# One rate for all four quarters: 16.4 units of product between the mixers' steps instead of 12.25, 14.25, 15.25 and 19.25

## The chip, the cores and the metric

The kernel runs on one core of a Trainium2 chip. The metric is the device time of one execution in microseconds (us). The program is built from Python: a kernel file issues instructions for five engines (TensorE, here PE; VectorE, DVE; ScalarE, ACT; GpSimd, POOL; SyncE, SP, which issues nearly all DMAs), and a scheduler decides in which order they stand in each engine's queue.

## The reference

One layer of a hybrid decoder on 2,048 prompt tokens and 8 single-token samples, D = 1024. Three mixers read one input projection and share one output projection; a SwiGLU follows.

```
h = rmsnorm(x, norm_mix);  p = h @ w_in                      # 1024 -> 31 column tiles of 128 (and 12 columns)
y_a = gated DeltaNet(p_a)     # 6 heads of 64, chunks of 64: u, w by a triangular solve, then s = s*g + k_dec^T v_new
y_b = RWKV-7(p_b)             # 6 heads: state update with a vector-valued decay
y_c = HGRN2(p_c)              # 4 heads, chunks of 64: o = q*exp(b) @ s + att @ v
x = x + concat(y_a, y_b, y_c) @ w_out                        # 8 input tiles of 128: 3 from A, 3 from B, 2 from C
h = rmsnorm(x, norm_ffn)
x = x + (silu(h @ w_gate) * (h @ w_up)) @ w_down             # 2816 = 22 tiles of 128
y = rmsnorm(x, norm_final)
```

All states after the prompt and after the sample step are returned too. Everything is float32; a product is made of three passes over halves that are rounded apart (`hi`, `lo`).

## The kernel before, in words

**Quarters.** The prompt's columns are cut into four quarters of 512 (the last has the 8 samples as well, 520). In names of tiles and below, quarters are numbered 0 to 3.

**Products.** `gemm()` in `emit` is one long generator: the input projections of quarters 0 to 3 (31 tiles each, PSUM tiles `psp`), then for each quarter in turn the output projection (`out_proj`, 8 tiles, `pso`), the gate and up products (`pfg`, `pfu`) and the down products (`pd`) in `ffn`. It yields the number of matmul rows of 512 columns that it has just issued, the unit of what follows: 24 for a tile of a projection, 48 for a gate and up pair, 12 for a tile of a down product. All in all there are 10,176 units. The input projections end at 2,976, and output projection and feed-forward of a quarter take 1,776: those of quarter 0 begin at 2,976, of quarter 1 at 4,752, of quarter 2 at 6,528, of quarter 3 at 8,304. Each matmul row of a product reads one weight tile and one 512-wide tile of inputs; three PSUM banks (pool `pg`) hold products in the making. In quarter 0 each weight is also split into its two halves on ACT and DVE and stored for the other quarters.

**Mixers.** A unit is one pair of heads of one mixer in one quarter, called g (DeltaNet, units 0 to 2), r (RWKV, 0 to 2) or h (HGRN2, 0 and 1) with quarter and unit: `h20` is the first HGRN2 unit of quarter 2. `gdn`, `rwkv` and `hgrn` return two generators, `first()` and `second()`; every `yield` in them ends a step, and `NEXT` passes the unit on to the next of four stages (preparation; the triangular inverse; the recurrence over 8 chunks; output and norm). At most 1, 1, 2 and 1 units are in the four stages (`ROOM`). At its end a unit writes a tile of 128 x 512 to memory (`store_mix`, into `s_mix`). In quarter 2 the eight units of the sample step (`gs`, `rs`, `hs`) join as side units in the last stage.

**What ties the two together.** `out_proj(q)` loads the eight tiles of `s_mix[q]` (`mxs`, from `g` 0 to 2, `r` 0 to 2, `h` 0 and 1), splits them on ACT and DVE, and multiplies them with `w_out`; tiles 6 and 7 come from `h` 0 and 1, whose units are the last of their quarter. Their last stage is `gated_norm`: a product `po_h` on PE, a sum over squares, a norm, a gate, the store.

**Who sets the order.** `Driver.turn` takes every live unit one step further; then it adds the quarter's rate to `due` and issues products until as many units are made:

```
        self.due += self.rate
        while self.made < self.due and self.product():
            pass
```

`RATES[q]` is that rate while units of quarter q are started. When all units are done the rest of the products follows alone (`K.late`, with more PSUM banks and weights loaded ahead). This is the order of the program. The scheduler then sets each engine's queue from it (`schedule_with_timeline_sim`), so that steps of mixers and products may stand further apart in a queue than the rate says. Each engine works through its queue in that order.

Of the kernel before, what the change touches and what calls it, by code (L numbers as in the profile page):

```python
# [1450 lines left out]
STEP = 2  # L1451
AHEAD = 4
SLACK = 6
RATES = (12.25, 14.25, 15.25, 19.25)
ROOM = (1, 1, 2, 1)

LANES = {"A": (29, 2, "A"), "I": (1, 0, "C"), "C": (2, 0, "C"), "D": (1, 0, "D"), "P": (6, 1, "P")}
# [58 lines left out]
def emit(K):  # L1516
# [61 lines left out]
    for q in range(4):  # L1578
        D.rate = RATES[q]
        for ms, f in order:  # L1580
# [118 lines left out]
```

## Time and profile before

| what | value |
|---|---|
| median of 3 runs | 3190.97 us (3185.88 to 3197.09) |
| the profiled execution | 3185.85 us, of which the span of its instructions is 3184.1 us |
| PE busy | 3063.0 us, 96% of the span, 24,812 matmul records |
| DVE busy | 2189.0 us, 69% |
| ACT busy | 1196.6 us, 38% |
| granted TensorE clock, mean | 0.985 of full speed |

Busy times are sums over records. Matmuls are pipelined and the ends of their records are modelled, so what one matmul costs in a row of others is read from the distance of two starts, not from its length. A float32 matmul that is not split into halves leaves two records. The granted clock 1.00 is the level of 2.4 GHz, 0.5 that of 1.2 GHz.

### The profile page before, as it was taken

The page shows a single profiled execution, that of the slowest core. Times are in us where ns is not written, and L with a number is a line of the kernel's source. Part 1 is how long each engine was busy: PE and PEld are TensorE (multiplying, and loading weights), DVE is VectorE, ACT ScalarE, POOL GpSimd, SP SyncE. Part 2 cuts the span into 40 slices and gives each one's busy share as a digit, 9 for nine tenths or more (in the row PEclk, how much of TensorE's full clock was granted, in tenths as well). Part 3 has the DMA queues.
Part 4 walks back from the last instruction along what each step waited for, and adds up shares of the span by engine and source line. Part 5 has one row for each costly group of instructions (what it writes and reads, how often), then busy time and mean ns, then how long its engine had stood idle before and what let it go on. Part 6 is the DMA issues. An engine that isn't in the chain of part 4 may idle for free.

```text
span 3184.1 us, 62691 instructions
## 1 busy us (share of the span) xinstructions
PE 3063.0 (96%) x24812; PEld 2442.2 (77%) x24812; DVE 2189.0 (69%) x5424; ACT 1196.6 (38%) x2064; POOL 12.3 (0%) x41
## 2 busy tenths in 40 slices
PE   7999999999998999999989999999999999999998
PEld 5767767778897677677766777777777777999998
DVE  6783666677768888896978778868877653443334
ACT  5452243245324544543555334445433221221002
POOL 0000000000000000000000000000000000000000
PEclk9999999999999999999999999999999999999999
DMA  8877666657656766677764454557554465755552
GB/s 286 287 244 250 193 182 199 207 168 228 185 164 172 235 229 221 223 221 257 226 219 149 153 163 146 190 165 233 165 162 150 151 216 183 251 170 186 189 182 90
DMA packets 391971, 628.01 MB, mean 197 GB/s; under 512 B 172988, under 2 KB 177340, under 8 KB 391676
## 3 DMA queue, kind: packets, MB, share of 16 engines
q1 hardware_dynamic: 390588, 622.93, 61.4%
q8 instruction: 195, 3.19, 0.4%
q10 hardware_dynamic: 1088, 1.07, 0.1%
q14 instruction: 100, 0.82, 0.1%
HBM read 456.77 MB, written 167.14 MB: 196 GB/s over the span
## 4 chain that ended last, share of the span: by engine, by line
PE 68%; DVE 13%; DMA 11%; ACT 4%; SPq 2%; issue 2%; DVEq 0%; ACTq 0%
PE psp L377 5%; PE psp L379 5%; PE psp L378 5%; PE pfg L378 4%; PE pfg L377 4%; PE pfg L379 4%; PE pfu L377 4%; PE pfu L378 4%; PE pfu L379 4%; PE pd L377 4%; PE pd L379 4%; PE pd L378 4%; PE pso L377 1%; PE pso L378 1%; PE pso L379 1%
## 5 line engine op out<-in xcount | busy, mean ns | idle before, releaser
L377 PE MATMUL psp<-xs,w_in 128*128 128x512 f32 (+1 forms) x1240 | 448.7, 362 | 23.8 <-ACT w_in L332 9.7
L378 PE MATMUL psp<-xs,w_in 128*128 128x512 f32 (+1 forms) x1240 | 444.1, 358 | 0.3 <-DVE xs L418 0.3
L379 PE MATMUL psp<-xs,w_in 128*128 128x512 f32 (+1 forms) x1240 | 443.6, 359 | 0.0
L377 PEld LDWEIGHTS psp<-xs,w_in 128*128 128x128 f32 x1240 | 236.6, 191 | 67.9 <-ACT w_in L332 11.2
L379 PEld LDWEIGHTS psp<-xs,w_in 128*128 128x128 f32 x1240 | 236.0, 190 | 41.7 <-issue 4.5
L378 PEld LDWEIGHTS psp<-xs,w_in 128*128 128x128 f32 x1240 | 236.5, 191 | 35.4 <-issue 2.0
L606 DVE TENSOR_TENSOR x<-pd,x 128x512 f32<-128x512 f32 (+1 forms) x240 | 137.5, 582 | 104.0 <-PE pd L379 102.6
L377 PE MATMUL pfg<-xhs,w_wg 128*128 128x512 f32 x464 | 188.2, 406 | 7.3 <-ACT w_wg L332 4.8
L378 PE MATMUL pfg<-xhs,w_wg 128*128 128x512 f32 x464 | 188.8, 407 | 3.1 <-DVE xhs L564 3.1
L377 PE MATMUL pd<-u,w_wd 128*128 128x512 f32 x448 | 179.3, 409 | 10.4 <-DVE x L606 7.0
L379 PE MATMUL pfg<-xhs,w_wg 128*128 128x512 f32 x464 | 187.1, 403 | 0.1
L377 PE MATMUL pfu<-xhs,w_wu 128*128 128x512 f32 x464 | 186.5, 402 | 0.0
L378 PE MATMUL pfu<-xhs,w_wu 128*128 128x512 f32 x464 | 186.3, 402 | 0.0
L379 PE MATMUL pfu<-xhs,w_wu 128*128 128x512 f32 x464 | 185.0, 399 | 0.0
L378 PE MATMUL pd<-u,w_wd 128*128 128x512 f32 x448 | 178.9, 400 | 0.6 <-DVE u L363 0.6
L379 PE MATMUL pd<-u,w_wd 128*128 128x512 f32 x448 | 178.9, 400 | 0.0
L585 ACT ACTIVATE t<-t 128x512 f32<-128x512 f32 (+1 forms) x110 | 60.0, 546 | 281.2 <-DVE t L584 277.5
L285 ACT ACT_TABLE_LOAD x91 | 116.8, 1283 | 112.6 <-PE yv_r L275 18.9
L362 ACT ACTIVATE u<-t 128x512 fp32r<-128x512 f32 (+1 forms) x110 | 60.0, 545 | 216.7 <-DVE t L588 216.7
L482 DVE TENSOR_TENSOR p<-psp,ri 128x512 f32<-128x512 f32 (+1 forms) x155 | 89.8, 580 | 71.8 <-PE psp L379 70.5
L377 PE MATMUL pd<-u,hw_wd 128*128 128x260 f32 (+1 forms) x432 | 128.2, 307 | 3.9 <-ACT u L362 3.9
L378 PE MATMUL pd<-u,hw_wd 128*128 128x260 f32 (+1 forms) x432 | 131.3, 305 | 0.0
(648 smaller groups left out, 7318.8 us busy)
## 6 DMA issues: line engine op xcount, KB each, us to landing
w_in<-sw_in SPq DMA_DIRECT2D x186, 512.0 KB
w_wg<-sw_wg SPq DMA_DIRECT2D x72, 512.0 KB
w_wu<-sw_wu SPq DMA_DIRECT2D x72, 512.0 KB
w_wd<-sw_wd SPq DMA_DIRECT2D x68, 512.0 KB
sw_in<-w_in SPq DMA_DIRECT2D x62, 512.0 KB
s_p<-p SPq DMA_DIRECT2D x93, 256.0 KB
sw_wg<-w_wg SPq DMA_DIRECT2D x44, 512.0 KB
sw_wu<-w_wu SPq DMA_DIRECT2D x44, 512.0 KB
```

The costliest lines, as they stand in the source:

```text
L285: p = self.nc.scalar.preload_act_table_set("natural_log_exp_and_others")
L362: nc.scalar.activation(out[:, 0], src, AF.Copy)
L377: nc.tensor.matmul(ps, lhsT=hi[:, ws], rhs=xs[:, 0, xc], start=start, stop=False)
L378: nc.tensor.matmul(ps, lhsT=hi[:, ws], rhs=xs[:, 1, xc], start=False, stop=False)
L379: nc.tensor.matmul(ps, lhsT=lo[:, ws], rhs=xs[:, 0, xc], start=False, stop=stop)
L482: nc.vector.tensor_tensor(p[:, c0:c0 + cn], ps, rstd[q][:, c0:c0 + cn], ALU.mult)
L585: nc.scalar.activation(t, g, AF.Tanh, scale=0.5)
L606: nc.vector.tensor_tensor(x2[d][:, c0:c0 + cn], ps, x2[d][:, c0:c0 + cn], ALU.add)
```

## The change

The four rates become one number. The mean of the four was 15.25; nothing else is edited.

```diff
 SLACK = 6
-RATES = (12.25, 14.25, 15.25, 19.25)
+RATES = (16.4, 16.4, 16.4, 16.4)
 ROOM = (1, 1, 2, 1)
```

The driver takes 484 turns with either. When the last unit is done, 7,536 units of product have been issued before, and 7,932 now. The counts of instructions are those of before on PE (19,008) and DVE (5,426); SP issues 2,315 instead of 2,343, since fewer weights are loaded in halves at the end.

Two places show what this does to the queues. The first is PE's queue at the output projection of quarter 2: `pso2_0` to `pso2_2` are its first three tiles, `mxs2_6` and `mxs2_7` the inputs that come from `h20` and `h21`. Before, the rows stand like this:

```order
L379 MATMUL pso2_0_25295<-mxs2_5_25277,w_o_0_2_25291 128x512
L377 MATMUL pso2_0_25295<-mxs2_6_25281,w_o_0_2_25291 128x512
L378 MATMUL pso2_0_25295<-mxs2_6_25281,w_o_0_2_25291 128x512
L379 MATMUL pso2_0_25295<-mxs2_6_25281,w_o_0_2_25291 128x512
L377 MATMUL pso2_0_25295<-mxs2_7_25285,w_o_0_2_25291 128x512
L378 MATMUL pso2_0_25295<-mxs2_7_25285,w_o_0_2_25291 128x512
L379 MATMUL pso2_0_25295<-mxs2_7_25285,w_o_0_2_25291 128x512
L377 MATMUL pso2_1_25349<-mxs2_0_25257,w_o_1_2_25343 128x512
```

The products follow each other without a mixer's row between them; `po_h20` and `po_h21` (16 rows each) stand 312 and 176 rows of products ahead of the first row that reads `mxs2_6`. Now the part where the input from `h20` is first read looks like this (`oss_h20` and `sp_hs00` are sums of the norm of `h20` and of the first HGRN2 sample unit, `g30`, `g31` and `r30` units of quarter 3):

```order
L378 MATMUL pso2_2_24326<-mxs2_5_24161,w_o_2_2_24322 128x512
L703 MATMUL pi_r30_23758<-uT_r30_23756,inF0_204 32x32 x7
L274 MATMUL oss_h20_22503<-hi_oss_h20_22504,blkr_92 128x512
L703 MATMUL pi_r30_23758<-uT_r30_23756,inF0_204 32x32 x6
L274 MATMUL ss_g31_23736<-hi_ss_g31_23737,blkr_92 128x512
L703 MATMUL pi_r30_23758<-uT_r30_23756,inF0_204 32x32 x7
L275 MATMUL oss_h20_22503<-lo_oss_h20_22505,blkr_92 128x512
L703 MATMUL pi_r30_23758<-uT_r30_23756,inF0_204 32x32 x12
L379 MATMUL pso2_2_24326<-mxs2_5_24161,w_o_2_2_24322 128x512
```

`po_h20` stands 23 product rows ahead of the first row that reads `mxs2_6`, and `po_h21` stands behind that row: between `po_h21` and the first row that reads `mxs2_7` there is no product at all. From the first row of `po_h20` to the first that reads `mxs2_7` PE's queue holds 244 rows now: 33 of products and 211 of mixers (400 records). The last rows ahead of `mxs2_7`:

```order
L1030 MATMUL paa_r31_24666<-wa3_22894,w2a2_113 128x512
L910 MATMUL pS_g30_24487<-Z0_g30_23305,kd_g30_22757 64x64
L910 MATMUL pS_g30_24487<-Z1_g30_23306,kd_g30_22757 64x64
L259 MATMUL pS_r30_24517<-SA_r30_24075,bt_r30_23583 64x64 x2
L377 MATMUL pso2_0_24179<-mxs2_7_24169,w_o_0_2_24175 128x512
L377 MATMUL pso2_1_24232<-mxs2_7_24169,w_o_1_2_24228 128x512
L377 MATMUL pso2_2_24326<-mxs2_7_24169,w_o_2_2_24322 128x512
```

All three banks of `pg` hold an unfinished tile there (`pso2_0`, `pso2_1`, `pso2_2`), so no other product can stand ahead of these rows.

The second place is SP's queue, where the stores of `h20` and `h21` and the loads that read them stand. Before:

```order
L759 DMA s_mix2_153<-y_h21_21610 128x512
L529 DMA mxs2_6_25281<-s_mix2_153 128x512
L347 DMA w_wd_5_1_1_25056<-sw_wd_5_1_0_1_19454 128x1024
L497 DMA pvr31_23894<-s_p3_150 128x513
L529 DMA mxs2_7_25285<-s_mix2_153 128x512
L1330 DMA o_hs<-S0_hs1_21637 128x8x64
L347 DMA w_wd_5_2_1_25115<-sw_wd_5_2_0_0_19524 128x1024
```

Behind these loads came weights (`w_wd`) of the down product of quarter 1, which is made ahead of the output projection of quarter 2. Now:

```order
L759 DMA s_mix2_153<-y_h21_22703 128x512
L497 DMA pvr31_24872<-s_p3_150 128x513
L529 DMA mxs2_7_24169<-s_mix2_153 128x512
L1330 DMA o_hs<-S0_hs1_22730 128x8x64
L1443 DMA o_gp<-st_g0_120 128x64
L347 DMA w_o_3_2_24391<-sw_o_3_0_1_11458 128x1024
```

The load `mxs2_7` follows its store two rows on, and the second half of the weights for the fourth tile (`w_o_3`) stands behind it. DVE's queue has 120 rows from the first that reads `po_h20` up to and with the split of `mxs2_7`: 58 of 512 elements, 12 of 256, 26 of 64 x 64 (the recurrences of `g30` and `r30`), 9 of 128 x 64 and 15 small ones. Between the last row that makes `y_h20` and the split of `mxs2_6` stand 13 of them, between `y_h21` and the split of `mxs2_7` 20.

Elsewhere the queues differ less than the rates: in the feed-forward of quarter 0 (units 2,976 to 4,752) PE's queue has 1,335 rows of mixers and samples instead of 1,403, in the input projection of quarter 3 (2,232 to 2,976) 619 instead of 823, and from unit 6,528 on 1,402 instead of 1,199. The last row of a mixer stands at unit 8,129 instead of 7,896, and `po_h31` at 8,098 instead of 7,865, both ahead of the output projection of quarter 3 at 8,304.

## Rows read from the trace of the kernel before

**Rows 1.** The profile's page: busy us, share of the span, instructions.

```profile
PE 3063.0 (96%) x24812; PEld 2442.2 (77%) x24812; DVE 2189.0 (69%) x5424; ACT 1196.6 (38%) x2064; POOL 12.3 (0%) x41
```

**Rows 2.** Busy us (and records) by stretch, then clock, DMA share, GB/s.

```profile
core 0: us, PE busy (x) PEld busy (x) DVE busy (x) ACT busy (x) POOL busy (x), PEclk, DMA share, GB/s
0.00:253.00 253.00, 224.53 (x1380) 166.10 (x1381) 190.10 (x433) 124.59 (x205) 2.51 (x21) 0.95 0.84 273
...
992.00:1040.00 48.00, 39.88 (x288) 30.03 (x288) 38.08 (x133) 22.89 (x47) 0.00 (x0) 0.86 0.61 156
1040.00:1600.00 560.00, 539.26 (x4334) 404.19 (x4336) 475.56 (x1133) 276.91 (x469) 1.05 (x2) 1.00 0.71 232
1600.00:1680.00 80.00, 69.42 (x503) 50.12 (x498) 62.24 (x144) 50.02 (x82) 0.00 (x0) 0.96 0.63 201
1680.00:2521.00 841.00, 829.77 (x6738) 621.99 (x6738) 651.80 (x1656) 345.18 (x582) 1.58 (x3) 1.00 0.52 167
2521.00:2640.00 119.00, 113.92 (x833) 87.63 (x831) 63.98 (x158) 32.29 (x46) 0.53 (x1) 1.00 0.62 207
2640.00:2800.00 160.00, 151.51 (x858) 132.71 (x858) 68.80 (x112) 33.29 (x51) 0.00 (x0) 0.97 0.61 204
2800.00:3120.00 320.00, 320.00 (x2677) 320.00 (x2676) 115.97 (x275) 38.10 (x85) 0.00 (x0) 1.00 0.56 183
```

**Rows 3.** PE's waits: for whom, us in total, times, longest.

```profile
PE psp L377 <- ACT w_in L332: 9.7, 4, 3.2
PE psp L377 <- ACT xs L417: 7.8, 2, 7.4
```

**Rows 4.** Line L377 alone, one of the products' three, 1680 to 2521 us.

```profile
1680.00:2521.00 841.00, 346.65 (x860) 161.85 (x860) 1.00 0.52 167
```

**Rows 5.** PE's timeline at the output projection of quarter 2: start, us.

```profile
2189.20 0.40 PE L379 MATMUL pd<-u,w_wd 128*128 128x512 f32 x1
2189.44 0.39 PE L377 MATMUL pso<-mxs,w_o 128*128 128x512 f32 x1
2189.67 0.40 PE L378 MATMUL pso<-mxs,w_o 128*128 128x512 f32 x1
```

**Rows 6.** Timelines of PE, DVE, SP and ACT, 2090 to 2172 us: `h20`, `h21`.

```profile
2095.42 1.15 PE L1284 MATMUL po_h<-W_h,Z_h 128*64 128x64 f32 x32
2139.05 1.15 PE L1284 MATMUL po_h<-W_h,Z_h 128*64 128x64 f32 x32
...
2114.27 0.75 DVE L939 SCALAR_TENSOR_TENSOR y_h<-y_h,derived,zs_h 128x512 f32<-128x512 f32 x1
...
2164.44 1.88 DVE L363 TENSOR_TENSOR mxs<-mxs 128x512 fp32r<-128x512 f32 x3
...
2171.09 0.69 DVE L363 TENSOR_TENSOR mxs<-mxs 128x512 fp32r<-128x512 f32 x1
...
2156.75 0.34 SPq L759 DMA_DIRECT2D s_mix<-y_h  x1
...
2163.56 0.32 SPq L529 DMA_DIRECT2D mxs<-s_mix  x1
...
2167.60 0.62 ACT L362 ACTIVATE mxs<-mxs 128x512 fp32r<-128x512 f32 x1
```

**Rows 7.** DVE groups by shape, 1680 to 2521 us: busy us, mean ns, idle before.

```profile
L913 DVE SCALAR_TENSOR_TENSOR Z_g<-Z_g,sg_g,pS_g 64x64 f32<-64x64 f32 x62 | 17.3, 279 | 9.7 <-PE pS_g L910 6.3 <-PE pv_r L259 2.8
L906 DVE COPY Z_g<-pv_g 64x64 f32<-64x64 f32 x68 | 15.1, 222 | 16.2 <-PE pv_g L904 9.1 <-PE pS_r L259 3.6 <-PE pl_h L1237 2.3
...
L900 DVE TENSOR_TENSOR X_g<-px_g,vb_g 128x64 f32<-128x64 f32 x35 | 7.6, 217 | 9.1 <-PE px_g L898 8.9
L864 DVE TENSOR_TENSOR Q_g<-pa_g,L_g 64x256 f32<-64x256 f32 x12 | 5.1, 422 | 0.2
```

**Rows 8.** PE's timeline at the output projection of quarter 0: start, us.

```profile
1024.71 0.63 PE L377 MATMUL pso<-mxs,w_o 128*128 128x512 f32 x1
1025.14 0.63 PE L378 MATMUL pso<-mxs,w_o 128*128 128x512 f32 x1
```

## The prediction, made before the changed kernel had run

> **What bounds the kernel now.** I began with the page's busy times. PE is busy 3063 us of a span of 3184.1, DVE 2189 [rows 1]; 121 us at most are idle on PE. The table by stretch says where: 8.1 us at 992 to 1040 (the output projection of quarter 0), 20.7 in the feed-forward of quarter 0 (1040 to 1600, DVE busy 85%), 10.6 at 1600 to 1680, but only 11.2 of 841 us from 1680 to 2521, where the last rate, 19.25, is at work, and 13.6 from 2521 to 2800, where the mixers end [rows 2]. From 2800 to 3120 products run alone without a gap. The list of PE's waits then shows that no single releaser costs more than 9.7 us in total [rows 3]. So PE sets the time nearly everywhere, and a mixer's row or a product's row costs PE about the same wherever it stands. What can move the time is idle time of PE alone.
>
> What a row costs PE, from starts that follow each other: 2189.44 to 2189.67, 0.233 us for a product's row of 512 columns [rows 5]. From 1680 to 2521 PE has three lines (L377 and its two neighbours) of 860 such rows each, 2,580 x 0.233 = 601 us [rows 4]; the other 6,738 - 2,580 = 4,158 records share the rest of the busy time, 229 us [rows 2], 0.055 us each.
>
> **What moves.** The number of turns (484), of products and of DVE's and PE's instructions stays. 396 units more are made by the last turn. They stood behind the mixers and now stand among them, and PE is full in either place: 0 us for the move itself.
>
> *The early quarters.* A rate of 16.4 instead of 12.25 or 14.25 should thin out the mixers, but the queues show little of it: the scheduler already put more products ahead than the rate said, and in the feed-forward of quarter 0 there are 5% fewer mixers' rows than before. That is where DVE is fullest. If its idle time fell to nothing, 20.7 us would be won; if it does not depend on the density, none. A stretch with DVE at 78% idles 1.3% of its time, one at 85% 3.7% [rows 2]; 5% fewer rows shift DVE by some 3 of these 7 points, so at most 3/7 of 2.4% of 560 us = 6 us. I take -3.
>
> *The end.* The mixers' last PE row moves from unit 7,896 to 8,129, still ahead of 8,304, where the output projection of quarter 3 begins. From `po_h31` to there are 206 product rows, 48 us, and the way from `po_h21` to the split of its tile took 2139.05 to 2171.78 = 33 us before [rows 6]: hidden. The waits at 2521 to 2800 [rows 2] may change by a little; -1, between -5 and +5.
>
> *Quarter 2's output projection.* This is the place that I expect to decide. Before, `po_h20` ran at 2095.42 and `po_h21` at 2139.05, the last input tile was split at 2171.78, and the output projection began at 2189.44 [rows 5, 6]: 17.7 us to spare. Now the output projection is reached earlier relative to the mixers: `po_h20` has 23 product rows left ahead of the first row that needs its result, and `po_h21` has none. PE must wait, since all three banks hold unfinished tiles. How long is bounded by DVE, whose 120 rows from `y_h20` to the split of `mxs2_7` must all be done between PE's `po_h20` and PE's first row on `mxs2_7`:
> - 58 rows of 512 at 0.63 us (three splits in 1.88 us [rows 6]) = 36.5
> - 12 of 256 at 0.42 = 5.0; 26 of 64 x 64 at 0.25 (between 0.279 and 0.222) = 6.5; 9 of 128 x 64 at 0.217 = 2.0 [rows 7]; 15 small ones at about 0.2 = 3.0
>
> Sum 53 us of DVE work. The store and the load cost more: from the issue of the store of `y_h` at 2156.75 to that of the load at 2163.56 and to its split at 2167.60 are 10.9 us [rows 6]; DVE has 13 rows (about 7 us) and 20 rows, mostly small (about 8 us), to do meanwhile, so it waits 3 to 4 us in the one case and 2 to 3 in the other, about 5. And the recurrences go to and fro between PE and DVE: the three groups show 9.7 + 16.2 + 9.1 = 35 us of idle ahead of 165 instructions [rows 7], 0.21 us each; 35 such rows make 7 us. Together 65 us from `po_h20` to the first row on `mxs2_7`.
>
> PE has in that time 33 product rows (7.7 us) and 400 records of mixers (22 us), 30 us. Idle: 65 - 30 = 35. From below: DVE's bare 53 - 30 = 23. From above: before, the same way took 2095.42 to 2171.78 = 76 us with products and samples between; 76 - 30 = 46. I take 34, near the middle. Nothing gives it back later: the mixers then stand ahead of where they were, but the stretches that follow had only 11.2 us of idle on PE to fill [rows 2], and PE must still make every product.
>
> Behind the waiting load on SP stands the second half of `w_o_3`. It is needed 9 + 12 product rows after `mxs2_7` (5 us), and a load took 4.0 us [rows 6]; 0, at most 2.
>
> *The clock.* After the wait at 992 to 1040 the output projection ran with starts 0.43 us apart, twice 0.233 [rows 5, 8], and the stretch had a granted clock of 0.86: 48 x 0.14 = 6.7 us [rows 2], part of it while PE idled. I take +3 for the new stall, between 0 and 7. The Trainium skill, in "TensorE: Matmul & The Clock Gate", section "Why this matters for your kernels", speaks against such a place more strongly: gaps between bursts of matmuls put the clock back to its lower level. By it each of the two waits (for `mxs2_6` and for `mxs2_7`) would be followed by such a stretch, which by the row at 0.86 would be up to 13 us and a total about 10 us above mine. The trace agrees so far that a stretch with 8.1 us of idle has one drop.
>
> Sum: +34 + 3 - 3 - 1 = +33 us on the profiled execution's own 3185.85, so 3219. That execution is the fastest of before; the median of the runs, 3190.97, is 0.16% above it, and a median would come to 3224 by the same sum. I say **3220**.
>
> **The rivals.**
> *No stall, no change.* If `h20` and `h21` get through on the chip in the 30 us that PE can fill, nothing is left but the move of 396 units, and the time is 3186 to 3191. For it: before, the chain had 17.7 us to spare, and DVE has fewer products' rows to do while PE stands. Against it: DVE's rows would have to take 30 us instead of 53, and they are queued in this order.
> *Faster.* The change may do what its words suggest: products between the mixers' steps cover their waits. In the Trainium skill, "Perfetto Trace Analysis", section "Optimization Strategy", says that a kernel whose bound changes over time may gain if its regimes are interleaved. By rows: of 53 us of idle at 992 to 1680 and 2521 to 2800 [rows 2] a third would go, 18 us, 3168, if also the stall were hidden. For it: DVE at 85% where PE idles most. Against: the same idle at 1680 to 2521 was lowest although DVE was at 78%, and the stall stands against it in any case.
> *A slower last quarter on top.* From unit 6,528 on 17% more mixers' rows stand among the products. If that lifts PE's idle from 1.3% to the 3.7% of the feed-forward of quarter 0 [rows 2], over the 1,601 units up to the last mixer (1,601 x 0.233 + about 150 = 520 us) it costs 12 us more: 3231. The stall works against it, since mixers get ahead in it.
>
> **How the numbers follow.** The stall as summed 0.68, with a slower last quarter 0.14, no stall 0.10, faster 0.08. 0.3% is 9.6 us, about what a measurement of this kernel can tell from no change. The stall's own lower end (+23, no clock, -6 and -5) is +12, at the edge of that, so I give no change 0.14, faster 0.07, slower 0.79. The stall's own range is 3198 to 3240; with the heavier case above and a part of the no-stall case below it becomes 3190 to 3246, which leaves out about 0.18.
>
> **What would show it.** In the profile of the changed kernel: two waits of PE on the splits of `mxs` (ACT or DVE, tiles `mxs`) at about 2130 to 2230 us, with PE idle 25 to 45 us inside some 70 us, where before it idled 11.2 us in all 841 [rows 2], DVE near full in it, and a drop of the granted clock behind it; the feed-forward of quarter 0 idle about as before; the stretch of products alone at the end shorter by about 50 us; no wait at the output projection of quarter 3. I am wrong if PE waits under 15 us at that place, or if the idle time of the other stretches moves by more than 10 us.

## The result, and the profile after

The change made the kernel faster by half a per cent: 3174.6 us (3170.44 to 3181.81) in the median of 9 runs, beside 3192.87 us (3185.88 to 3197.09) of before in as many; the ratio is 0.9949, with a 95% interval of 0.9936 to 0.9961. The prediction was 3220 us, between 3190 and 3246. The profiled execution after took 3181.53 us, near the slow end of its runs, that of before 3185.85, the fastest of its own; so the traces differ by 4.4 us of span, the medians by 18. What is read from the two traces below adds up to the 4.4; the other 14 us of the medians' difference stand in neither, and where they lie is not shown.

The page of the kernel after, busy times as in [rows 1]:

```profile
span 3179.7 us, 62651 instructions
PE 3063.7 (96%) x24812; PEld 2445.6 (77%) x24812; DVE 2198.8 (69%) x5424; ACT 1197.5 (38%) x2063; POOL 12.5 (0%) x41
```

PE's busy time is the same, and its idle time is 116 us instead of 121. That hides two large moves of opposite sign. Stretches of equal time no longer hold equal work, so both traces are cut where the same product rows begin: units 372 (the mixers start), 2,976, 4,752, 6,528, 6,720 (end of the output projection of quarter 2), 7,600 and 8,304. The kernel before by these stretches, columns as in [rows 2]:

```profile
126.90:1022.10 895.20, 862.66 (x7947) 683.49 (x7945) 616.46 (x1642) 329.44 (x593) 2.15 (x13) 0.98 0.66 201
1022.10:1602.80 580.70, 559.93 (x4429) 419.05 (x4430) 490.55 (x1182) 287.37 (x486) 1.05 (x2) 0.99 0.71 231
1602.80:2189.40 586.60, 567.91 (x4353) 425.49 (x4352) 469.15 (x1175) 275.64 (x466) 1.05 (x2) 0.99 0.54 172
2189.40:2252.20 62.80, 62.80 (x597) 47.91 (x596) 43.43 (x99) 26.67 (x44) 0.00 (x0) 1.00 0.66 206
2252.20:2543.00 290.80, 287.68 (x2423) 212.91 (x2422) 213.43 (x559) 101.54 (x168) 1.05 (x2) 0.99 0.49 157
2543.00:2735.90 192.90, 183.91 (x1064) 145.36 (x1063) 93.17 (x186) 42.77 (x62) 0.00 (x0) 0.98 0.60 200
```

The kernel after, by the same units, and products alone at the end:

```profile
129.30:987.40 858.10, 836.63 (x7671) 666.10 (x7669) 585.94 (x1547) 302.49 (x550) 2.30 (x13) 0.99 0.68 208
987.40:1568.60 581.20, 556.52 (x4183) 414.94 (x4184) 476.25 (x1110) 289.61 (x479) 1.05 (x2) 0.97 0.70 229
1568.60:2143.30 574.70, 566.64 (x4493) 431.67 (x4492) 469.79 (x1203) 254.25 (x436) 1.05 (x2) 0.99 0.55 173
2143.30:2251.90 108.60, 90.72 (x831) 63.63 (x829) 81.23 (x199) 64.58 (x110) 0.00 (x0) 0.80 0.53 161
2251.90:2542.00 290.10, 284.60 (x2415) 211.81 (x2409) 210.70 (x539) 96.58 (x160) 0.53 (x1) 0.99 0.48 153
2542.00:2732.50 190.50, 190.50 (x1226) 149.12 (x1226) 112.25 (x246) 56.80 (x83) 0.53 (x1) 1.00 0.61 207
...
2800.00:3120.00 320.00, 320.00 (x2676) 320.00 (x2676) 117.41 (x279) 34.47 (x81) 0.00 (x0) 1.00 0.57 184
```

The output projection of quarter 2 (fourth row) took 108.6 us instead of 62.8: the predicted wait is there. But it began 46 us earlier, at 2143.3 instead of 2189.4; the input projections (first row) are 37 us shorter, 858.1 instead of 895.2, with 276 records fewer, and the stretch from 4,752 to 6,528 is 12 us shorter. The mixers' end (last row but one) lost its 9 us of idle time although it has 162 records more.

Since mixers' records move between stretches too, I take their work off. A product's row counts 0.2275 us (0.1195 with 260 columns), any other record the mean distance of starts of its line in these two traces. This work is 2865.9 us in every kernel, because all have the same records and each has one price; what a stretch takes beyond it is called its **loss** here: idle time, half-speed clock, and rows that stand farther apart than usual. Before 308.7 us, after 304.2. The price of a product's row is a low one (the median distance of two starts is 0.233 us); since a stretch holds the same product rows in every kernel, differences of losses do not depend on it.

PE's timeline after at the output projection of quarter 2, to be read beside [rows 5] (in brackets the idle time ahead and what ended it):

```profile
2151.86 1.15 PE L1284 MATMUL po_h<-W_h,Z_h 128*64 128x64 f32 x32
...
2163.57 0.33 PE L898 MATMUL px_g<-Z_g,kb_g 64*64 64x64 f32 x4 [1.78 <-DVE uT_r L704]
2165.33 1.15 PE L710 MATMUL pj_r<-inD,uT_r 32*32 32x32 f32 x64 [1.42 <-DVE X_g L900]
...
2175.10 1.65 PE L377 MATMUL pso<-mxs,w_o 128*128 128x512 f32 x3 [1.03 <-ACT mxs L362]
...
2185.85 1.15 PE L1284 MATMUL po_h<-W_h,Z_h 128*64 128x64 f32 x32
2190.09 0.50 PE L274 MATMUL oss_h<-hi_oss_h,blkr 128*128 128x512 f32 x1 [1.68 <-ACT hi_oss_h L272]
2193.71 0.80 PE L275 MATMUL oss_h<-lo_oss_h,blkr 128*128 128x512 f32 x1 [3.13 <-DVE lo_oss_h L273]
2196.39 0.37 PE L910 MATMUL pS_g<-Z_g,kd_g 64*64 64x64 f32 x2 [1.46 <-DVE Z_g L906]
...
2207.80 1.65 PE L377 MATMUL pso<-mxs,w_o 128*128 128x512 f32 x3 [0.46 <-ACT mxs L362]
```

From `po_h20` (2151.86) to the first row on `mxs2_7` (2207.80) are 55.9 us. The wait is no single gap: PE goes to and fro with DVE through the recurrences that stand ahead of `mxs2_7`, and the longest gap is 3.13 us. On the splits of `mxs` themselves PE waits 2.3 us in all (1.5 on ACT's half, 0.8 on DVE's). The largest of PE's waits from 2143.3 to 2251.9, as in [rows 3], and the one on ACT's half:

```profile
PE oss_h L275 <- DVE lo_oss_h L273: 3.1, 1, 3.1
...
PE pso L377 <- ACT mxs L362: 1.5, 2, 1.0
```

The stretch from `po_h20` on, cut at the steps of the clock:

```profile
2151.90:2164.70 12.80, 10.22 (x133) 7.37 (x132) 9.53 (x19) 12.62 (x20) 0.00 (x0) 1.00 0.69 215
2164.70:2181.80 17.10, 12.47 (x152) 7.92 (x152) 15.35 (x29) 11.56 (x20) 0.00 (x0) 0.50 0.47 148
2181.80:2192.00 10.20, 6.24 (x103) 4.99 (x99) 9.57 (x26) 7.99 (x16) 0.00 (x0) 1.00 0.01 2
2192.00:2219.40 27.40, 20.80 (x77) 11.55 (x78) 26.05 (x74) 14.19 (x23) 0.00 (x0) 0.50 0.51 144
2219.40:2251.90 32.50, 32.38 (x335) 25.34 (x333) 16.93 (x44) 17.52 (x30) 0.00 (x0) 1.00 0.64 201
```

The clock stood at 1.2 GHz twice, for 17.1 and 27.4 us, 44.5 us in all. PE was idle 17.9 us in the whole stretch (fourth row of the kernel after: 108.60 - 90.72), 11.2 of them in these two pieces. It was thus busy at 1.2 GHz for 33.3 us, and half of that, 16.6 us, is what the clock cost at most; with the idle time that is 34.5 of the loss of 38.1 us. DVE was busy 90 to 95% of each piece from 2164.7 to 2219.4.

### The profile page after: what moved, and what is told of

It reads as the page before. It is cut to its first block, busy times and chain, and to the rows that moved or that the text cites. A ratio compares the mean times of both kernels' runs of the same rounds, so it can differ in the third digit from the quotient of the medians.

```text
span 3179.7 us, 62651 instructions
## 1 busy us (share of the span) xinstructions
PE 3063.7 (96%) x24812; PEld 2445.6 (77%) x24812; DVE 2198.8 (69%) x5424; ACT 1197.5 (38%) x2063; POOL 12.5 (0%) x41
## 4 chain that ended last, share of the span: by engine, by line
PE 72%; DVE 12%; DMA 9%; ACT 4%; issue 2%; SPq 2%; DVEq 0%; ACTq 0%
PE psp L377 5%; PE psp L378 5%; PE psp L379 5%; PE pd L377 5%; PE pd L379 5%; PE pfu L377 5%; PE pd L378 5%; PE pfu L379 5%; PE pfg L377 4%; PE pfu L378 4%; PE pfg L378 4%; PE pfg L379 4%; DMA rw_in<-w 2%; PE pso L379 1%; PE pso L378 1%
## 5 line engine op out<-in xcount | busy, mean ns | idle before, releaser
L377 PE MATMUL psp<-xs,w_in 128*128 128x512 f32 (+1 forms) x1240 | 447.2, 361 | 21.6 <-ACT xs L417 8.9
L377 PEld LDWEIGHTS psp<-xs,w_in 128*128 128x128 f32 x1240 | 235.2, 190 | 67.8 <-ACT w_in L332 10.3
L377 PE MATMUL pd<-u,w_wd 128*128 128x512 f32 x496 | 202.0, 414 | 10.0 <-DVE x L606 6.7
L378 PE MATMUL pfg<-xhs,w_wg 128*128 128x512 f32 x496 | 202.6, 408 | 3.7 <-DVE xhs L564 3.6
L377 PE MATMUL pfg<-xhs,w_wg 128*128 128x512 f32 x496 | 202.0, 407 | 0.2
L377 PE MATMUL pfu<-xhs,w_wu 128*128 128x512 f32 x496 | 200.5, 404 | 0.5 <-ACT w_wu L332 0.5
L378 PE MATMUL pd<-u,w_wd 128*128 128x512 f32 x496 | 200.4, 405 | 0.0
L379 PE MATMUL pd<-u,w_wd 128*128 128x512 f32 x496 | 199.1, 403 | 0.0
L379 PE MATMUL pfg<-xhs,w_wg 128*128 128x512 f32 x496 | 199.1, 401 | 0.0
L379 PE MATMUL pfu<-xhs,w_wu 128*128 128x512 f32 x496 | 198.9, 401 | 0.0
L378 PE MATMUL pfu<-xhs,w_wu 128*128 128x512 f32 x496 | 198.3, 400 | 0.0
L377 PEld LDWEIGHTS pd<-u,w_wd 128*128 128x128 f32 x496 | 94.2, 191 | 34.9 <-DVE x L606 3.0
L587 DVE SCALAR_TENSOR_TENSOR t<-pfu,rf 128x512 f32<-128x512 f32 (+1 forms) x110 | 64.1, 583 | 77.8 <-PE pfu L379 74.7
```

Source lines behind the costliest of these rows:

```text
L377: nc.tensor.matmul(ps, lhsT=hi[:, ws], rhs=xs[:, 0, xc], start=start, stop=False)
L378: nc.tensor.matmul(ps, lhsT=hi[:, ws], rhs=xs[:, 1, xc], start=False, stop=False)
L379: nc.tensor.matmul(ps, lhsT=lo[:, ws], rhs=xs[:, 0, xc], start=False, stop=stop)
L587: nc.vector.scalar_tensor_tensor(p, psu, 0.5, r[:, cs], ALU.mult, ALU.mult)
```

## The experiments

The kernel before, run beside these, had medians between 3191.8 and 3197.6 us. First the loss (us) of every kernel by stretch, worked out as above from its profiled execution; the first column after the name holds units 0 to 372, the others begin at the unit named.

```
kernel        0   372  2976  4752  6528  6720  7600  8304 |  sum | ratio to before (95%)
before     34.1  96.4  63.8  58.5   2.6  24.2  17.7  11.4 | 308.7 |
after      36.5  73.5  74.1  40.5  38.1  26.4   4.9  10.2 | 304.2 | 0.9949 (0.9936, 0.9961)
e1         34.3  75.5  63.4  61.1   5.8  18.5   7.1  10.5 | 276.2 | 0.9876 (0.9852, 0.9899)
e2         36.4  81.9  64.1  51.9   2.1  13.4   4.5  10.9 | 265.3 | 0.9857 (0.9831, 0.9884)
e3         35.2  78.8  68.3  48.9   3.4  42.3  16.9  11.4 | 305.2 | 0.9962 (0.9951, 0.9973)
e4         33.6  71.7  66.7  49.2   4.0  18.7   8.5  11.2 | 263.5 | 0.9842 (0.9817, 0.9868)
e5         36.1 104.2  66.7  58.8   2.6  23.7   6.8  13.2 | 312.2 | 0.9967 (0.9940, 0.9994)
e6         37.0 100.2  65.0  44.1   5.4  17.7  17.8  11.4 | 298.6 | 0.9939 (0.9917, 0.9962)
e7         35.3  78.3  66.0  51.4   3.4  17.6   6.8   9.3 | 268.1 | 0.9853 (0.9831, 0.9874)
e8         33.4  76.8  68.9  49.8   4.6  18.5   5.4  11.4 | 268.8 | 0.9822 (0.9801, 0.9844)
e9         35.7  73.4  78.8  64.2  12.0  17.3   6.0  11.2 | 298.7 | 0.9952 (0.9934, 0.9970)
e10        33.1  73.3  64.9  45.0  41.4  16.1   8.8  12.1 | 294.7 | 0.9948 (0.9934, 0.9963)
e11        38.7  92.9  82.6  53.8   3.5  29.7   3.8  10.7 | 315.7 | 1.0002 (0.9989, 1.0015)
e12        33.6  74.2  73.3  43.2   3.8  24.4   9.3  67.0 | 328.8 | 1.0039 (1.0026, 1.0051)
```

How well a loss repeats is seen in e5, whose PE queue is that of before up to unit 7,680: 2.0, 7.8, 2.9, 0.3, 0.0 and -0.5 us apart. In the input projections e2 and e11, whose mixers' records stand there in the same windows of 24 units but for 8 of 4,692, are even 11.0 us apart; from 2,976 to 6,528 the other pairs with one queue (e3 and e7, e4 and e8) are at most 2.5 apart.

**e1: the first rate alone.**

```diff
-RATES = (12.25, 14.25, 15.25, 19.25)
+RATES = (16.4, 14.25, 15.25, 19.25)
```

> Rates 16.4, 14.25, 15.25, 19.25: only the first quarter's rate is raised. In the queues no wait at the output projection of quarter 2 (131 product rows stand between po_h21 and the first row on its tile). Theory A (the changed kernel's gain comes from the early stretches: it lost 23 us less than before in the input projections, beyond the mixers' rows that it had not yet done): 3170, faster by about 20 us. Theory B (the gain comes from the lower last rate, through the end of the mixers, where the changed kernel lost 13 us less): no change, 3193. Theory C (no rate matters beyond the places where a queue happens to wait): 3185 to 3193.

3153.1 us (3150.7 to 3154.03): more than twice the gain of the whole change, from one of its four numbers. The input projections of before (first row of its stretches above) answer to this row of e1:

```profile
127.10:1001.00 873.90, 853.74 (x7939) 677.56 (x7937) 619.69 (x1649) 320.56 (x582) 2.14 (x13) 1.00 0.66 206
```

No theory gave so much: theory A had 20 us. The first rate alone also lowers the loss from 6,720 to 8,304, by 16 us. In the input projections, with nearly the same records (7,939 and 7,947), PE was idle 20.2 us instead of 32.5, and half of the time at 1.2 GHz is 3 us instead of 16.

**e2: all rates up in proportion, to the same mean of about 16.4.**

```diff
-RATES = (12.25, 14.25, 15.25, 19.25)
+RATES = (13.17, 15.32, 16.4, 20.7)
```

> Rates 13.17, 15.32, 16.4, 20.7: more products in all, in the old proportion; the last mixer's row stands at unit 8215 and no wait is to be seen in the queues at the output projection of quarter 2. Theory A (early rates): a small gain, 3183 to 3188, since the first rate rises by a quarter of what the change did. Theory B (the lower last rate): slower, 3195 to 3205. If more products among the mixers paid in themselves (396 units or more moved from the end): 3175 or less.

3146.6 us (3142.93 to 3151.44). No wait at quarter 2, and less loss in four stretches at once, the input projections (14 us less) and the two from 6,720 (24 less) above all. Of the three outcomes put down beforehand it is the last, that more products among the mixers pay in themselves; which of its four rates did it is not shown.

**e3: one rate, the old mean.**

```diff
-RATES = (12.25, 14.25, 15.25, 19.25)
+RATES = (15.25, 15.25, 15.25, 15.25)
```

> Rates 15.25 in all quarters: equal, with the old mean. The last mixers' rows stand in a row of 154 without a product at unit 7536, where the products after the mixers begin. Theory A (early rates): 15 to 20 us gained early, 5 to 15 us lost at that row of 154: 3175 to 3190. Theory B (lower last rate): 3170 or less, since the last rate falls most. No change if neither matters.

3180.6 us (3178.54 to 3183.51), as theory A had it: the input projections won 18 us, nothing waits at quarter 2, and units 6,720 to 7,600 took 18 us more, somewhat over the 5 to 15 expected there. The 154 mixers' rows without a product stand in PE's queue at unit 7,536. A stretch at that place, columns as in [rows 2]:

```profile
2507.00:2530.00 23.00, 13.80 (x206) 11.20 (x207) 21.62 (x67) 3.91 (x7) 0.00 (x0) 0.50 0.19 64
```

and PE's waits from 2507 to 2560, as in [rows 3]:

```profile
PE pl_h L1237 <- DVE att_h L1240: 4.8, 5, 2.2
PE pv_r L259 <- DVE X_r L1121: 4.0, 1, 4.0
```

It is a wait like that of quarter 2, in another place: DVE busy 21.6 of 23 us, PE 13.8, and at 1.2 GHz. This led to e5 and e7.

**e4: more among the mixers, without the wait.**

```diff
-RATES = (16.4, 16.4, 16.4, 16.4)
+RATES = (16.4, 15.25, 15.25, 17.5)
```

In its queue 221 and 92 product rows stand between `po_h20`, `po_h21` and their readers.

> Rates 16.4, 15.25, 15.25, 17.5: the early rise and a lower last rate, but at the output projection of quarter 2 221 and 92 product rows stand between po_h20, po_h21 and the first rows on their tiles, so that PE need not wait there. If the wait cost what the comparison of the traces says (35 us of PE that did neither products nor mixers in units 6528 to 6720): 3140 to 3150. If the wait is given back later, because the mixers that ran in it are done: 3170 to 3178, as the changed kernel.

3141.8 us (3138.51 to 3146.59), 33 us below the changed kernel and inside the range for a wait that is not given back. The output projection of quarter 2, to be read beside the fourth rows above:

```profile
2152.90:2215.80 62.90, 61.35 (x480) 45.32 (x479) 54.01 (x140) 34.22 (x57) 0.00 (x0) 1.00 0.74 243
```

**e5: the switch at the end later.** When the last unit is done, six more tiles of product follow, and then the late mode begins (`K.late`), in which products take the mixers' PSUM banks. The program runs ahead of the queues, so at that point mixers' rows still stand in them.

```diff
-SLACK = 6
+SLACK = 20
```

> The kernel before with SLACK 20 instead of 6: the same queue on PE up to unit 7,680, and behind it the switch to the late mode (in which products take the mixers' PSUM banks) comes 14 tiles of product later, when the last mixers' rows are through. Theory L (a switch while mixers' rows still stand in the queues makes PE wait at the end of the mixers, where the kernel before lost 16 us between units 7,600 and 8,000 and the changed one 3): the time falls by 10 to 13 us, to 3180 to 3184, and the loss in units 7,600 to 8,000 to about 4. Rival (the mixers' last chains are slow wherever the switch stands, and the changed kernel only had more products left to cover them): within 3 us of before, 3190 to 3197.

3188.6 us, ratio 0.9967, where the kernel before, run beside it, had 3197.6; the time lies between the ranges of the two theories. The end of the mixers in the kernel before, PE's waits from unit 7,600 to 8,304:

```profile
PE pd L377 <- ACT u L362: 3.9, 1, 3.9
PE pfu L377 <- ACT osq_h L296: 2.1, 1, 2.1
```

A gate and up product (`pfu`) waits there for a mixer's norm (`osq_h`) to let go of a bank. In e5 both waits are gone, and idle time falls from 9.0 to 1.5 us:

```profile
2555.70:2737.60 181.90, 180.43 (x1064) 142.91 (x1063) 94.19 (x186) 42.60 (x62) 0.00 (x0) 1.00 0.62 213
```

The loss falls by 10.9 us there, as theory L had it; the whole time by 0.33%, 10.5 us (by its interval 2 to 19).

**e6: the first rate alone put back.**

```diff
-RATES = (16.4, 16.4, 16.4, 16.4)
+RATES = (12.25, 16.4, 16.4, 16.4)
```

> The changed kernel with its first rate alone put back, 12.25 (16.4 for the other three). No wait at the output projection of quarter 2 in its queue (343 and 194 product rows between po_h20, po_h21 and their readers), last mixer's row at unit 7,896 as before. Theory F (what was won away from that wait was won with the first rate: without it the first quarter's input projection, the start of output projection 1 and the end of the mixers cost what they cost before): 3183 to 3193. Rival (more products among the mixers pay wherever they are added; with the wait gone too): 3145 to 3160.

3176.9 us (ratio 0.9939), between the two theories and nearer to F. Nothing waits at quarter 2 (5.4), yet it is no faster than the changed kernel: the input projections are back at 100.2 and the end of the mixers at 17.8.

**e7: e3 with the later switch.**

```diff
-SLACK = 6
-RATES = (12.25, 14.25, 15.25, 19.25)
+SLACK = 20
+RATES = (15.25, 15.25, 15.25, 15.25)
```

> Four rates of 15.25 as in the run with the same mean (3180.6), with SLACK 20 instead of 6: the run of 154 mixers' rows without a product at unit 7,536 is gone from PE's queue. Theory L: the 47 us that were lost there between units 7,200 and 8,000 fall to about 12, and the time to 3143 to 3150. Rival (the chains cost the same wherever): 3172 to 3181.

3150.5 us, 30 less than e3, close to what theory L gave. The run of 154 rows was made by the switch, it is gone from the queue of e7, and the two last stretches of the mixers fell from 59 us of loss to 24.

**e8: e4 with more products among the last mixers.**

```diff
-RATES = (16.4, 16.4, 16.4, 16.4)
+RATES = (16.4, 15.25, 15.25, 18.5)
```

> The kernel without the wait (16.4, 15.25, 15.25, 17.5: 3141.8) with a last rate of 18.5: more products among the last mixers still (last mixer's row at unit 8,137 instead of 8,089), and no new wait in the queue (221 and 92 rows at output projection 2, 268 and 209 at output projection 3). If more products among the mixers pay by themselves: 3134 to 3140. If the gain lay in the places named (first projection, start of output projection 1, end of the mixers), which this queue has won already: 3139 to 3146.

3139.4 us (3137.85 to 3146.59), ratio 0.9822: the fastest kernel here, 1.8% below before, but not told apart from e4 (0.9842 with an overlapping interval), and in the range of both theories, which it does not decide.

**e9: the second rate alone put back.**

```diff
-RATES = (16.4, 16.4, 16.4, 16.4)
+RATES = (16.4, 14.25, 16.4, 16.4)
```

> The changed kernel with its second rate alone put back (16.4, 14.25, 16.4, 16.4). The queue's wait at the output projection of quarter 2 is gone (257 and 132 product rows ahead of the readers), the input projections of quarters 1 and 2 and the last rate are as in the changed kernel. Theory (the wait costs its 33 to 38 us on top of what was won, and the lower last rate costs nothing): 3137 to 3142, or up to 3155 if the switch to the late mode, which now meets the mixers' rows at unit 7,938 as they end, costs its 13 us again. Rival (what is won elsewhere is won because PE waits there, so that the mixers get ahead): 3170 to 3185.

3177.4 us, which looks like the rival, but the stretches say that it isn't: the loss at quarter 2 falls by 26 us, to 12 (a smaller wait is left there, with PE idle 5.5 us, which I had not expected), and what cancels it stands ahead of that place, 24 us more in units 4,752 to 6,528 and 5 in those before, where the second rate has changed the queue. A wait cannot act on what stands ahead of it. The time alone would have misled here; one number was put back, and three stretches changed.

**e10: e8 with a first rate of 18.**

```diff
-RATES = (16.4, 15.25, 15.25, 18.5)
+RATES = (18, 15.25, 15.25, 18.5)
```

> The fastest kernel so far (16.4, 15.25, 15.25, 18.5: 3139.4) with a first rate of 18. Its queue has the wait at the output projection of quarter 2 again (36 and 1 product rows ahead of the readers) and a nearer one at quarter 3 (86 and 76). Theory (the wait costs 30 to 40 us whichever rates bring it): 3168 to 3182, with the granted clock below 0.9 and PE idle 12 to 20 us in units 6,528 to 6,720. Rival (more products in the first quarter still pay, as they did from 12.25 to 16.4, by more than the wait costs): 3130 to 3150.

3175.3 us, 36 above e8. The wait is back, with 41.4 us of loss against 4.6 and PE idle 21.8 us, a little over what I had said. The input projections win 3.5 us more, less than one queue varies by there:

```profile
2135.40:2246.00 110.60, 88.80 (x795) 62.16 (x796) 79.88 (x201) 59.29 (x99) 0.00 (x0) 0.78 0.52 155
```

**e11: the first rate at 14.25.**

```diff
-RATES = (12.25, 14.25, 15.25, 19.25)
+RATES = (14.25, 14.25, 15.25, 19.25)
```

> The kernel before with its first rate alone raised to 14.25 instead of 16.4. Its queue in units 372 to 744 has the same 298 mixers' rows as before (256 with 16.4), in all input projections 2,396 instead of 2,382; last mixer's row at unit 7,868. If what the first rate wins goes by its size (40 us for 4.15 more): 3170 to 3178. If it goes by the rows that the scheduler in fact moves there: within 8 us of before, 3185 to 3200.

3192.2 us, no change (1.0002). In units 372 to 744 its loss is 18.9 us, with the same 298 mixers' rows as before (18.8); with 256 rows it is 9.9 in the changed kernel and 10.8 in e1. So it is in all kernels: with 298 rows the loss there is 18 to 20 us (12.25, 13.17 and 14.25 as first rate), with fewer 9 to 12 (15.25 and more). What counts is what the scheduler does with the rate. The rest of its table is mixed: 14 us won at the end, 19 lost in units 2,976 to 4,752.

**e12: the changed kernel, with the wait removed in another way.**

```diff
-            if q == 2:
+            if q == 3:
                 D.side(samples.pop(0), 3)
```

> The changed kernel with its four rates of 16.4, whose sample units join in quarter 3 instead of quarter 2. Its queue has the same mixers' rows as the changed kernel up to unit 4,752; po_h20 and po_h21 then stand 446 and 388 product rows ahead of their readers, so the wait at the output projection of quarter 2 is gone with nothing ahead of it changed, but po_h30 and po_h31 stand only 11 and 22 ahead of theirs at unit 8,304. Theory (the wait costs its 35 us on top of what was won elsewhere): loss in units 6,528 to 6,720 of 2 to 6 us instead of 38, in units 372 to 4,752 within 8 us of the changed kernel's; the time 3140 to 3150 if no wait comes at 8,304, and up to 3170 if one comes there. Rival (PE's wait there lets the mixers get ahead and is given back behind it): 3168 to 3180 with no wait at either place.

3208.9 us (3203.54 to 3211.75), slower than the changed kernel, and outside what either theory gave: I had put a wait at quarter 3 at some 20 to 30 us, and it costs 57. The question was answered all the same. Up to unit 4,752 every stretch is within 3 us of the changed kernel's; the output projection of quarter 2 is back at a loss of 3.8 instead of 38.1; and behind it nothing is dearer by 34 us until the new wait at unit 8,304. The two places in e12:

```profile
2132.60:2188.10 55.50, 55.44 (x389) 41.54 (x388) 35.90 (x94) 21.47 (x37) 0.00 (x0) 1.00 0.74 239
2691.10:2790.00 98.90, 52.99 (x325) 44.95 (x324) 45.27 (x81) 34.48 (x55) 0.00 (x0) 0.67 0.39 117
```

and PE's waits in the second:

```profile
PE pso L377 <- ACT mxs L362: 9.6, 3, 5.2
PE mo_hs L274 <- ACT hi_mo_hs L272: 5.9, 2, 3.0
PE sp_hs L274 <- ACT hi_sp_hs L272: 5.2, 2, 2.6
```

There three sample units (`rs2`, `hs0`, `hs1`) stand between the readers of `mxs3_5`, `mxs3_6` and `mxs3_7`. They are chains of small steps without recurrences beside them, so PE has less to do in this wait than in that of quarter 2 and idles 46 of 99 us.

## Why the prediction was wrong

**Quarter 2's output projection: right in place; in price by luck, as two errors cancel.** It was put at +34 for the wait and +3 for the clock, 37 together. The table gives 38.1 - 2.6 = 35.5; e10 against e8 36.8; e12 against the changed kernel 34.3. The way from `po_h20` to `mxs2_7` took 55.9 us, not 65: nearly the bare work of DVE that was its lower bound, 53 us (DVE was busy 49.8 us in it). Idle time was half of what I said (17.9 instead of 34; I had named 25 to 45 as the sign), and the clock cost five times as much (up to 16.6 instead of 3). The Trainium skill's "TensorE: Matmul & The Clock Gate", section "Why this matters for your kernels", pointed the right way for the clock: gaps between bursts put it back. I read that as one drop behind each wait; the trace has two drops, of 17.1 and 27.4 us, but they begin at 2164.7 and 2192.0, ahead of the rows on the two tiles (2175.1 and 2207.8), in the to and fro with DVE. The total does not come out 10 us above mine, because only half of the idle time that I had put beside the clock was there.

**No giving back: right.** Behind the wait, units 6,720 to 8,304 lost 31.3 us after and 41.9 before, but those 11 us are not the wait's doing: e1, e4, e8 and e10, with and without the wait, have 24 to 27 there.

**What failed: "0 us for the move itself", with "What can move the time is idle time of PE alone".** The work is the same in each kernel, but what PE loses beside it is not. Away from the wait 304.2 - 38.1 = 266 us were lost instead of 306, 40 less. Of these 23 are idle time, 2 clock (half of the time at 1.2 GHz), and the remaining 15 lie in time in which PE counts as busy, its rows standing farther apart. I had 53 us of idle time in view and allowed 4 of it to go; my own second sign of being wrong, idle time elsewhere moving by more than 10 us, came true.

**Early quarters, -3 (0 to -6): the step with the largest error.** I compared how many mixers' rows stand in the feed-forward of quarter 0, found 5% fewer, and let DVE's idle share set the price. That stretch became dearer by 10 us. The gain came ahead of it, in the input projections, which the prediction did not cost at all: 96.4 to 73.5, of it 11 us idle time and 10 clock. That the first rate does this is shown by e1 and e6, one part alone and that part undone: in the three kernels with 12.25 (before, e5 and e6, which have one PE queue there) this loss is 96 to 104 us, in the nine with 15.25 or more 72 to 79. By which wait it does so stays open, since PE's waits there are many and small; the largest group of before, for loads of `w_in`, fell by 3.2 us (first line before, 126.9 to 1022.1 us, second line after, 129.3 to 987.4):

```profile
PE psp L377 <- DMA w_in<-sw_in: 6.0, 5, 1.8
PE psp L377 <- DMA w_in<-sw_in: 2.8, 3, 1.2
```

Units 4,752 to 6,528 won 18 us more, and the table shows the rate that did it, the second: with 14.25 the loss there is 54 to 64 us (five kernels), with 15.25 or 15.32 45 to 52 (six), with 16.4 40 to 44 (three). Against the changed kernel e9, which puts back that number alone, loses 23.7 us there; e6, which puts back the first, only 3.6. Through which wait stays open here too. For the 10 lost in the feed-forward of quarter 0 I have no cause, and across the kernels, from 63 to 83, no order by any one rate; of what kind they are can be read: the clock stood at 1.2 GHz for 30 us there instead of 10, and PE was idle 24.7 us instead of 20.8.

**The end, -1 (±5): -12.8.** The mechanism was missed, not only its size. I asked whether the mixers end ahead of the output projection of quarter 3, which they do. What costs is the late mode that begins while mixers' rows still stand in the queues; e5 and e7, which move only the switch, show it (10.9 and 35 us). With 396 units more made by the last turn the changed kernel switches behind most of those rows: by its trace 70 records of mixers stand behind that point (unit 8,004), while before 238 stood behind it (unit 7,680).

**`w_o_3`, 0 to 2: right.** PE waits for no load of it.

**The rivals.** "Faster" gave 3168, nearest to the 3174.6 measured, but on the condition that the wait be hidden; it was not, and twice what that rival allowed was won elsewhere, so that its number is near by luck. e8, where the wait is gone, is that rival come true, with 3139. "No stall" and "a slower last quarter" did not happen. The sum by steps, in the profiled executions: input projections -22.9, units 2,976 to 4,752 +10.3, to 6,528 -18.0, the wait +35.5, to 7,600 +2.2, to 8,304 -12.8, the first and last stretches +1.2: -4.5 us, the difference of the spans but for 0.1. So the change is the sum of a wait that was foreseen, of three gains that were not (by the first rate, by the second, and by the later switch), and of 10 us lost without a named cause.

## What to carry to other kernels

Where a change of order moves the work of a whole program, the length of a wait that is seen in the queue can be bounded from the engine that must get through its rows first (53 us of work, 55.9 measured); but it is one term, and the stretches where the order changes without a visible wait moved by 10 to 23 us each here, in both directions. Such a sum needs their loss per stretch of equal work, before any of them is put at nothing, and the same queue traced twice, to see how far a loss repeats (here within 11 us in the longest stretch and 3 us in the next two). Look for switches in the program (here the late mode) whose place depends on how far the queues lag behind it; to judge one part of such a change, compare stretches, not times: e9's time spoke for the wrong theory.

## What the hardware showed unexpectedly

The granted clock fell to 1.2 GHz in a wait that has no long gap. Ahead of the first fall, at 2164.7, PE was idle in two gaps, of 1.78 us and of 0.80 up to the fall, with four records of 64x64 matmuls between them; ahead of the second, at 2192.0, in gaps of 1.68 us and of 1.4 up to the fall, with one matmul of 512 columns between them. The longest gap of the whole wait is 3.13 us. The clock stood at that level for 44.5 us in all; what that cost, 16.6 us by PE's busy time in it, is nearly as much as the 17.9 us of idle time. In the input projections the same is seen on a smaller scale: of the 23 us between before and after, 10 are half of the time at 1.2 GHz.
